# Down products one expert behind the gate and up products, loads in that order, and the last h2 rows written ahead of the last output store

## The chip, the cores and the metric

The kernel runs on one core of a Trainium2 chip. Its engines are PE (matmul), DVE (VectorE), ACT (ScalarE), POOL (GpSimd) and SP (SyncE, which here only issues transfers); each works through its own list of instructions in order and waits on semaphores for the others. Sixteen DMA engines move the data. The metric is the time of one execution on the device in microseconds, the median of the runs shown.

## The reference, cut to what matters

One layer of a streaming encoder for 512 prompt rows and 64 sample rows (576 in all, model width 1024): attention of two kinds, an output projection with its residual, and then a hierarchical mixture of experts, in which the whole change lies:

```python
h2 = RMSNorm(x) * (1 + scale2) + shift2
x  = x + gate2 * HierMoE(h2)

g_sel = argmax(n @ w_rg + b_rg)                    # one of 4 groups
e_logits = (n @ w_re + b_re).reshape(-1, 4, 8)     # 8 experts in each
top_val, top_i = top_k(e_in_group, 2)
w_top = softmax(top_val) * p_group
for e in range(32):
    act = silu(n @ w_e_gate[e]) * (n @ w_e_up[e])  # 1024 -> 256
    out = out + combine[:, e:e + 1] * (act @ w_e_down[e])   # 256 -> 1024
```

## The kernel before, in words

The rows stand in tiles of 128 (four of prompt rows, t = 0 to 3, and one of 64 sample rows). After the output projection each tile gets its residual `y[t]`, which `store_rows(t)` writes to the output `y`, and its normed rows h2, which `keep_h2(t)` writes to a scratch array `h_d` in DRAM. Both writes are issued by ACT. The router then makes, for each of 32 experts, a table of at most 64 rows: `gidx` (rows of `h_d` to gather, a column for each pair of experts), `sidx` (half rows of the output, a column for each expert) and the weights `wslot`. `weight_table` and `overflow_blocks` go on to make the table of what lies beyond 64 rows; this one goes through DVE, an IOTA on POOL and two small writes by ACT, `ov_d` and `ovf_d`.

For a pair of experts `clear_rows` (a copy on ACT) zeroes a tile `xg`, `gather_rows` (an indirect DMA that POOL issues) fetches 128 rows of `h_d`, and `turned_rows` transposes them: eight PE transposes into `pxg`, copied to `xT` in two halves, by ACT (line 90) and by DVE (line 92). For one expert there follow

- the gate and up products, tile `gu`: eight steps of four matmuls with `weg` and `weu` (line 1602);
- silu on ACT and a product on DVE, tile `sl` (lines 1606 and 1607);
- two transposes `ta` on PE and their copy `aT` on ACT (lines 1612 and 1614);
- the down products, tile `dn`, with `wed` (line 1619), times the gains `gw` (`row_gains`, lines 1593 and 1594) and added on DVE to the 128 half rows `yr`;
- `take_rows`, issued before that, gathers those half rows from the output, and `put_rows` scatters them back, both indirect DMAs of POOL (lines 1637 and 1643). A take follows in the program the writes that it may depend on, the stores of `y` among them.

Each expert has three weight tiles of 1 MB, `weg`, `weu` and `wed`. They go through a ring of 20 tiles, which is filled before the expert loop begins; `next_tile` hands out the next tile of the ring in the order expert 0's three, expert 1's three and so on, SP issues its load (line 1488), and it waits both for a free slot and for the landing of an earlier load.

The order on every engine is written by hand: the functions are called in program order, and inside the expert loop `expert_parts` is a generator that `begin` runs a few steps at a time. Of expert e+1 three steps of products run, then ta of expert e, two more steps, then dn of expert e, and then the three left of e+1. The last two tiles of `wed` are loaded together (`held`). Ahead of the loop come the gather of pair 0, `weight_table`, `overflow_blocks`, `turned_rows` of pair 0, the gather of pair 1, the takes of experts 0 and 1, and the products of expert 0.

Of the kernel before, what the change touches and what calls it, by code (L numbers as in the profile page):

```python
# [26 lines left out]
KD = 8  # L27
# [5 lines left out]
NE = 32  # L33
# [14 lines left out]
def body(ctx, tc, I, O):  # L48
# [1418 lines left out]

    shapes = (("weg", wg_, KD, FE), ("weu", wu_, KD, FE), ("wed", wd_, 2, D))
# [11 lines left out]
    def next_tile():  # L1480
        e, i = divmod(turnstile[0], 3)
        w = ring_tile(shapes[i][2], shapes[i][3], shapes[i][0])
        ahead.setdefault(e, []).append(in_halves(w, shapes[i][2]))
        return pieces_of(w, e % 4 * 8 + e // 4, i)
# [112 lines left out]
    def expert_parts(xT, w, wp, ws, yr):  # L1597
        gu = s_ps("gu")
        gw = row_gains(wp, ws)
        for k in range(KD):  # L1600
            for j in range(2):
                pe.matmul(gu[64 * j:64 * j + 64, 0:FE], xT[:, k], w[j][k // 4][:, k % 4, :],  # L1602
                          start=(k == 0), stop=(k == KD - 1))
            yield
        sl = work.tile([128, FE], F32, name="sl", tag="yh", bufs=3)
        act.activation(sl[64:128], gu[0:64, 0:FE], AF.Silu)  # L1606
        dve.tensor_mul(sl[64:128], sl[64:128], gu[64:128, 0:FE])
        yield
# [6 lines left out]
        yield  # L1615
# [33 lines left out]
    with tc.manual_schedule(engines=ENG):  # L1649
# [104 lines left out]
        store_rows(3)  # L1754
# [15 lines left out]
        keep_h2(3)  # L1770
        for _ in range(9):
            steps(chain, 1)
            steps(chain4, 1)
# [12 lines left out]
        steps(slot)  # L1786
        steps(weights)
        Z_cm.__exit__(None, None, None)
        Ep = ctx.enter_context(tc.tile_pool(name="Ep", bufs=2))
        ovrow = Ep.tile([1, 24, 4], I32, name="ovrow", bufs=1)  # L1790
        weight_table()
        overflow_blocks()
        xT = turned_rows(xg, 128)
        xg = clear_rows()
        gather_rows(xg, gidx[:, 1:2], 128)
        yrs = {e: take_rows(sidx[:, e:e + 1], e) for e in range(2)}

        def parts_of(e):
            j = 64 * (e % 2)
            return expert_parts(xT[:, :, j:j + 64], ahead[e], wslot[:, 0, e:e + 1], wslot[:, 1, e:e + 1], yrs[e])  # L1800

        e0 = parts_of(0)
        steps(e0, KD + 2)
    held = []

    def load_next(e):
        for i in range(3 * e + 20, 3 * e + 23):
            if i == 3 * (NE - 2) + 2:
                held.extend(next_tile())
            elif i == 3 * NE - 1:  # L1810
                load(held)
                load_tiles(1)
            elif i < 3 * NE:
                load_tiles(1)

    with tc.manual_schedule(engines=ENG):
        steps(e0)
        put_rows(yrs[0], sidx[:, 0:1], 0)
        load_next(0)
        begun = {0: iter(())}  # L1820
        nxt = [turned_rows(xg, 128)]

        def begin(e, n):
            nonlocal xT
            if e < NE and e not in begun:
                if e % 2 == 0:
                    xT = nxt.pop()
                begun[e] = parts_of(e)
            if e < NE:
                steps(begun[e], n)  # L1830

        def rows_ahead(e):
            if e < NE:
                yrs[e] = take_rows(sidx[:, e:e + 1], e)

        xg = clear_rows()
        gather_rows(xg, gidx[:, 2:3], 128)
        rows_ahead(2)
        begin(1, 3 + 2)
        for e in range(1, NE):  # L1840
            begin(e, KD + 1 - 3 - 2)
            begin(e + 1, 3)
            begin(e, 1)
            begin(e + 1, 2 if e < NE - 2 else KD + 1 - 3)
            begin(e, 9)
            put_rows(yrs[e], sidx[:, e:e + 1], e)
            load_next(e)
            if e == NE - 2:
                begin(e + 1, 9)
                put_rows(yrs[e + 1], sidx[:, e + 1:e + 2], e + 1)  # L1850
                break
            if e % 2 == 0:
                nxt.append(turned_rows(xg, 128))
                m = e // 2 + 2
                if m < NE // 2:
                    xg = clear_rows()
                    gather_rows(xg, gidx[:, m:m + 1], 128)
            rows_ahead(e + 2)
            if e == 8:
                act.dma_start(ovrow, ov_d[0:24].rearrange("(o a) b -> o a b", o=1))  # L1860

    nov = nc.values_load(ovrow[0:1, 0, 2:3], min_val=0, max_val=MAXOV,
                         skip_runtime_bounds_check_because="at most 1152 routed rows in blocks of 64")
    with tc.For_i(0, nov, 1) as it:
# [27 lines left out]
        steps(expert_parts(xT[:, :, 0:64], load_expert(bass.ds(ent, 1)), wsl[:, 0], wsl[:, 1], yr))  # L1892
# [49 lines left out]
```

## Time and profile before

| | us |
|---|---|
| median of 3 runs | 894.48 |
| lowest, highest | 893.54, 895.44 |
| the profiled execution | 895.09 |
| its span | 893.1 |
| PE busy in the span | 796.2 (89%) |
| DVE busy | 534.2 (60%) |
| ACT busy | 310.8 (35%) |
| POOL busy | 289.1 (32%) |

The span is what the profiler sees of the program, from its first to its last instruction; the profiled execution lasts 2.0 us longer. Its own time is 0.6 us above the median. The kernel moves 195 MB in the span, and half of that is the 96 tiles of 1024 KB of the experts' weights. The busy times are shares of the whole span, over stages of different kinds, so they don't tell what limits the experts.

### The profile page before, as it was taken

The numbers are of one execution on the slowest core, as the hardware profiler recorded it, in microseconds if no ns is written. First come the engines' busy times: TensorE is split into PE (matmuls) and PEld (weight loads), VectorE is DVE, ScalarE is ACT, GpSimd is POOL, SyncE is SP. The second block draws the span as 40 slices with busy tenths as digits, with TensorE's granted clock in tenths as the row PEclk, the third lists the DMA queues.
The fourth block names the chain that finished last, engine by engine and source line by source line (L and its number), as shares of the span: only waits on it lengthen the run. The fifth ranks groups of instructions, "written<-read, shape, count | busy, mean of one in ns | idle before, by whom it ended". The sixth has DMA issues, their size and how long they took to land.

```text
span 893.1 us, 16227 instructions
## 1 busy us (share of the span) xinstructions
PE 796.2 (89%) x6108; PEld 627.2 (70%) x6108; DVE 534.2 (60%) x1285; ACT 310.8 (35%) x754; POOL 289.1 (32%) x380
## 2 busy tenths in 40 slices
PE   6799999999899978999999999985799998878883
PEld 3567897877689967869999999984455554444441
DVE  3458999878956988647052445498355444342441
ACT  4363322475533546557232323432212212111210
POOL 1551432254447740412010103441233343332321
PEclk9899999999999989999999999996799999999997
DMA  9956778321012300126233129989699999999980
GB/s 307 344 168 217 263 242 297 104 62 61 17 61 88 108 4 2 49 97 172 71 95 95 49 97 345 350 301 405 186 415 414 413 412 407 415 413 401 416 333 36
DMA packets 78530, 194.95 MB, mean 218 GB/s; under 512 B 13587, under 2 KB 48387, under 8 KB 66419
## 3 DMA queue, kind: packets, MB, share of 16 engines
q1 hardware_dynamic: 68768, 174.85, 53.6%
q0 software_dynamic: 7424, 14.18, 4.7%
q10 hardware_dynamic: 2258, 4.87, 1.4%
q8 instruction: 49, 0.80, 0.4%
q14 instruction: 31, 0.25, 0.1%
HBM read 186.86 MB, written 18.01 MB: 229 GB/s over the span
## 4 chain that ended last, share of the span: by engine, by line
PE 46%; DMA 24%; DVE 18%; issue 5%; ACT 3%; POOL 2%; SPq 1%; POOLq 0%; DVEq 0%; ACTq 0%
DMA weu<-in_w_e_up 11%; DMA yr<-out_y,sidx 4%; PE pg L410 4%; PE pg L412 4%; PE pg L411 4%; PE gu L1602 3%; PE pj L215 3%; PE pj L217 3%; PE pj L216 3%; DVE K L904 2%; DVE acc L683 2%; DVE m L682 2%; DMA xg<-h_d,gidx 2%; DMA weg<-in_w_e_gate 2%; PE o L799 2%
## 5 line engine op out<-in xcount | busy, mean ns | idle before, releaser
L1602 PE MATMUL gu<-weu,xT 128*64 128x256 f32 x512 | 133.4, 402 | 21.7 <-DMA weu<-in_w_e_up 21.7
L1602 PE MATMUL gu<-weg,xT 128*64 128x256 f32 x512 | 132.2, 398 | 0.5 <-ACT sl L1606 0.5
L215 PE MATMUL pj<-whi,hT 128*128 128x256 f32 (+1 forms) x352 | 107.3, 305 | 0.9 <-DVE yn L472 0.6
L217 PE MATMUL pj<-whi,hT 128*128 128x256 f32 (+1 forms) x352 | 100.7, 286 | 1.3 <-DVE hT L234 1.3
L216 PE MATMUL pj<-wlo,hT 128*128 128x256 f32 (+1 forms) x352 | 100.5, 286 | 0.0
L1602 PEld LDWEIGHTS gu<-weg,xT 128*64 128x64 f32 x512 | 66.6, 141 | 40.8 <-issue 13.3
L203 DVE TENSOR_TENSOR wlo<-raw,whi 128x512 fp32r<-128x512 f32 (+1 forms) x72 | 53.5, 764 | 68.4 <-ACT whi L202 67.8
L1602 PEld LDWEIGHTS gu<-weu,xT 128*64 128x64 f32 x512 | 67.8, 142 | 33.7 <-DMA weu<-in_w_e_up 27.6
L1621 DVE TENSOR_TENSOR gw<-gw,dn 128x512 f32<-128x512 f32 x32 | 22.0, 688 | 105.6 <-PE dn L1619 105.6
L1643 POOL DMA_INDIRECT out_y<-yr,sidx x32 | 33.7, 1053 | 148.2 <-DVE yr L1622 139.2
L410 PE MATMUL pg<-hT,whi 128*128 128x256 f32 (+1 forms) x256 | 78.3, 306 | 0.0
L412 PE MATMUL pg<-hT,whi 128*128 128x256 f32 (+1 forms) x256 | 75.7, 296 | 0.0
L411 PE MATMUL pg<-hT,wlo 128*128 128x256 f32 (+1 forms) x256 | 75.7, 296 | 0.0
L215 PEld LDWEIGHTS pj<-whi,hT 128*128 128x128 f32 x352 | 67.1, 190 | 8.1 <-issue 4.9
L217 PEld LDWEIGHTS pj<-whi,hT 128*128 128x128 f32 x352 | 66.6, 189 | 1.6 <-DVE hT L234 1.5
L216 PEld LDWEIGHTS pj<-wlo,hT 128*128 128x128 f32 x352 | 66.9, 190 | 0.1
L203 POOL TENSOR_TENSOR wlo<-raw,whi 128x512 fp32r<-128x512 f32 (+1 forms) x32 | 41.9, 1332 | 74.2 <-ACT whi L202 54.4
L202 ACT CAST whi<-raw 128x512 fp32r<-128x512 f32 (+1 forms) x104 | 60.3, 624 | 14.8 <-PE pu L1134 14.8
L1619 PE MATMUL dn<-wed,aT 128*64 128x512 f32 x256 | 60.5, 594 | 0.8 <-ACT aT L1614 0.8
L410 PEld LDWEIGHTS pg<-hT,whi 128*128 128x128 f32 x256 | 48.5, 189 | 4.6 <-issue 4.3
L906 POOL TENSOR_TENSOR B<-B,K 128x512 f32<-128x512 f32 (+4 forms) x36 | 35.5, 985 | 41.5 <-DVE K L904 29.2
L411 PEld LDWEIGHTS pg<-hT,wlo 128*128 128x128 f32 x256 | 48.5, 190 | 0.2
(392 smaller groups left out, 2026.4 us busy)
## 6 DMA issues: line engine op xcount, KB each, us to landing
weg<-in_w_e_gate SPq DMA_DIRECT2D x26, 1024.0 KB, 16.5
weu<-in_w_e_up SPq DMA_DIRECT2D x26, 1024.0 KB, 21.6
wed<-in_w_e_down SPq DMA_DIRECT2D x26, 1024.0 KB, 18.5
raw<-in_w_in SPq DMA_DIRECT2D x20, 1024.0 KB, 5.6
wa<-in_w_ada SPq DMA_DIRECT2D x16, 512.0 KB, 10.6
va<-in_w_ada SPq DMA_DIRECT2D x8, 1024.0 KB, 5.3
obT<-in_w_ada SPq DMA_DIRECT2D x8, 1024.0 KB, 6.7
weg<-in_w_e_gate SPq DMA_DIRECT2D x12, 512.0 KB, 11.1
```

The source lines that it names most:

```text
L202: act.copy(hi[:, a:a + 2], raw[:, a:a + 2])
L203: eng.tensor_tensor(lo[:, a:a + 2], raw[:, a:a + 2], hi[:, a:a + 2].bitcast(F32), op=ALU.subtract)
L215: pe.matmul(p[:, :n], a, hi[:, k, :], start=(k == 0), stop=False)
L216: pe.matmul(p[:, :n], a, lo[:, k, :], start=False, stop=False)
L217: pe.matmul(p[:, :n], b, hi[:, k, :], start=False, stop=(k == KD - 1))
L410: pe.matmul(p[:, :b - a], hi[:, k, cs], hT[:, k, a:b], start=(k == 0), stop=False)
L411: pe.matmul(p[:, :b - a], lo[:, k, cs], hT[:, k, a:b], start=False, stop=False)
L412: pe.matmul(p[:, :b - a], hi[:, k, cs], hT[:, k, LP + a:LP + b], start=False, stop=(k == KD - 1))
L906: pool.tensor_tensor(B[:, :nk], B[:, :nk], K[:, 1:nk + 1], op=ALU.mult)
L1602: pe.matmul(gu[64 * j:64 * j + 64, 0:FE], xT[:, k], w[j][k // 4][:, k % 4, :], start=(k == 0), stop=(k == KD - 1))
L1619: pe.matmul(dn[64 * j:64 * j + 64, :], aT[:, k, :], w[2][k][:, 0, j * 512:(j + 1) * 512], start=(k == 0), stop=(k == 1))
L1643: ordered(pool.indirect_dma_start(out=y_rows, out_offset=bass.IndirectOffsetOnAxis(ap=idx_ap, axis=0), in_=yr, in_offset=None, bounds_chec ...
```

## The change

A list `sequence` sets the order of the ring: gate and up tiles of expert e, then the down tile of expert e-1. The generator is cut into `expert_up`, `expert_turn` and `expert_down`. The loop now runs for expert e: all products of `gu`; after an odd expert the transposes of the next pair's rows; dn and the put of expert e-1; the gains of e+1; ta of expert e; two or three loads; after an odd expert the next gather; the take of expert e+2. `held` is gone, and the loads end in the same order as before. Ahead of the loop the takes of experts 0 and 1 and the gather of pair 1 stand before `weight_table` and `overflow_blocks`, and in the program before them. `store_rows(3)` stands behind `keep_h2(3)`. Line numbers below 1468 stay, those of the helpers grow by about five.

```diff
+    sequence = [(0, 0), (0, 1)]
+    for e in range(1, NE):
+        sequence += [(e, 0), (e, 1), (e - 1, 2)]
+    sequence.append((NE - 1, 2))
...
     def next_tile():
-        e, i = divmod(turnstile[0], 3)
+        e, i = sequence[turnstile[0]]
...
-        store_rows(3)
         steps(chain, 6)
...
         xg = clear_rows()
         keep_h2(3)
+        store_rows(3)
...
         gather_rows(xg, gidx[:, 0:1], 128)
         row_indices(rowc, NE, sidx)
-        steps(slot)
-        steps(weights)
         Z_cm.__exit__(None, None, None)
...
+        yrs = {e: take_rows(sidx[:, e:e + 1], e) for e in range(2)}
+        steps(slot)
+        steps(weights)
+        xg1 = clear_rows()
+        gather_rows(xg1, gidx[:, 1:2], 128)
         weight_table()
         overflow_blocks()
         xT = turned_rows(xg, 128)
-        xg = clear_rows()
-        gather_rows(xg, gidx[:, 1:2], 128)
-        yrs = {e: take_rows(sidx[:, e:e + 1], e) for e in range(2)}
...
+        def down(e):
+            expert_down(aTs.pop(e), ahead.pop(e), gws.pop(e), yrs[e])
+            put_rows(yrs.pop(e), sidx[:, e:e + 1], e)
+
+        gain_rows(0)
+        for e in range(NE):
             j = 64 * (e % 2)
...
-        for e in range(1, NE):
-            begin(e, KD + 1 - 3 - 2)
-            begin(e + 1, 3)
-            begin(e, 1)
-            begin(e + 1, 2 if e < NE - 2 else KD + 1 - 3)
-            begin(e, 9)
-            put_rows(yrs[e], sidx[:, e:e + 1], e)
-            load_next(e)
...
+            sl = expert_up(xT[:, :, j:j + 64], ahead[e])
+            if e % 2 and e < NE - 1:
+                xT = turned_rows(xg, 128)
                 m = e // 2 + 2
                 if m < NE // 2:
                     xg = clear_rows()
-                    gather_rows(xg, gidx[:, m:m + 1], 128)
-            rows_ahead(e + 2)
+            if e:
+                down(e - 1)
+            gain_rows(e + 1)
+            aTs[e] = expert_turn(sl)
+            for _ in range(2 if e == 0 else 3):
+                if turnstile[0] < len(sequence):
+                    load_tiles(1)
+            if e % 2 and e < NE - 1 and m < NE // 2:
+                gather_rows(xg, gidx[:, m:m + 1], 128)
+            if e + 2 < NE:
+                yrs[e + 2] = take_rows(sidx[:, e + 2:e + 3], e + 2)
...
+        down(NE - 1)
```

POOL, at the entry to the expert stage. Its list before (`xg<-h_d` is a gather, `yr<-out_y` a take, `out_y<-yr` a put, `IOTA rq` the step of `overflow_blocks`):

```order
L1573 DMA xg<-h_d,gidx 128x1024
L1555 IOTA rq 128x32
L1573 DMA xg<-h_d,gidx 128x1024
L1637 DMA yr<-out_y,sidx 128x512 x2
L1643 DMA out_y<-yr,sidx 1152x512
```

And after, at the same place:

```order
L1578 DMA xg<-h_d,gidx 128x1024
L1644 DMA yr<-out_y,sidx 128x512 x3
L1578 DMA xg<-h_d,gidx 128x1024
L1560 IOTA rq 128x32
L1650 DMA out_y<-yr,sidx 1152x512
```

Three takes and the gather of pair 1 have moved ahead of the IOTA, on which the issues of `ov_d` and `ovf_d` depend.

ACT, in the same stretch, before (`R` is a step of the router's softmax, `xg<-zero` is `clear_rows`):

```order
L1411 ACTIVATE R<-R 128x5
L1564 DMA ov_d<-ovi 128x4
L1565 DMA ovf_d<-ovf 128x1
L90 COPY xT<-pxg 128x512
L1569 COPY xg<-zero_82 128x1024
L1606 ACT_TABLE_LOAD
```

And after:

```order
L1411 ACTIVATE R<-R 128x5
L1574 COPY xg<-zero_82 128x1024
L1569 DMA ov_d<-ovi 128x4
L1570 DMA ovf_d<-ovf 128x1
L90 COPY xT<-pxg 128x512
L1609 ACT_TABLE_LOAD
```

The zeroing of pair 1's tile has moved ahead; the copy of `xT` for expert 0 still stands behind the two small writes.

PE, near the end, before, with buffer numbers: the last row of the products of expert 30 (`gu_9364`), the first six of expert 31 (`gu_9405`), and ta of expert 30:

```order
L1602 MATMUL gu_9364<-weu_9086,xT_9338 64x256
L1602 MATMUL gu_9405<-weg_9131,xT_9338 64x256
L1602 MATMUL gu_9405<-weu_9133,xT_9338 64x256
L1602 MATMUL gu_9405<-weg_9131,xT_9338 64x256
L1602 MATMUL gu_9405<-weu_9133,xT_9338 64x256
L1602 MATMUL gu_9405<-weg_9131,xT_9338 64x256
L1602 MATMUL gu_9405<-weu_9133,xT_9338 64x256
L1612 MATMUL ta_9414<-ident_72,sl_9402 128x64 x2
```

And after: the last row of the products of expert 30 (`gu_9375`), dn of expert 29, ta of expert 30, and the first two rows of the products of expert 31 (`gu_9412`):

```order
L1606 MATMUL gu_9375<-weu_9059,xT_9341 64x256
L1626 MATMUL dn_9395<-wed_9105,aT_9369 64x512 x2
L1626 MATMUL dn_9395<-wed_9106,aT_9369 64x512 x2
L1617 MATMUL ta_9407<-ident_72,sl_9392 128x64 x2
L1606 MATMUL gu_9412<-weg_9109,xT_9341 64x256
L1606 MATMUL gu_9412<-weu_9111,xT_9341 64x256
```

So ta of expert 30 no longer stands among the products of expert 31, whose sixteen rows now stand in one piece. In both kernels dn of expert 30, ta and dn of expert 31 follow them and end the list.

## Rows read from the trace of the kernel before

**Rows 1.** Windows: length; PE, PEld, DVE, ACT, POOL busy (x); clock; DMA share; GB/s.
```profile
600.00:625.00 25.00, 13.89 (x133) 12.64 (x133) 21.70 (x108) 6.58 (x14) 6.28 (x8) 0.68 1.00 404
...
650.00:850.00 200.00, 177.45 (x1198) 94.16 (x1196) 86.92 (x143) 36.55 (x78) 71.48 (x65) 0.97 1.02 412
```

**Rows 2.** Waits from 600 us: us in total, times, longest us.
```profile
PE gu L1602 <- DMA weu<-in_w_e_up: 21.7, 11, 3.1
```

**Rows 3.** Timeline of SP's issues: start, us, line, transfer.
```profile
638.10 0.33 SPq L1488 DMA_DIRECT2D wed<-in_w_e_down  x1
...
856.06 0.33 SPq L1488 DMA_DIRECT2D wed<-in_w_e_down  x1
```

**Rows 4.** Timeline of PE, products of expert 0, first and last two pairs.
```profile
632.54 0.69 PE L1602 MATMUL gu<-weg,xT 128*64 128x256 f32 x1
...
637.48 0.38 PE L1602 MATMUL gu<-weg,xT 128*64 128x256 f32 x1
...
637.69 0.38 PE L1602 MATMUL gu<-weg,xT 128*64 128x256 f32 x1
```

**Rows 5.** Timeline of PE, the tail: end of the last weu wait, ta, dn.
```profile
870.89 0.43 PE L1602 MATMUL gu<-weu,xT 128*64 128x256 f32 x1 [1.02 <-DMA weu<-in_w_e_up]
...
872.34 0.45 PE L1612 MATMUL ta<-ident,sl 64*128 64x64 f32 x2
872.72 0.43 PE L1602 MATMUL gu<-weg,xT 128*64 128x256 f32 x1
...
874.93 1.89 PE L1619 MATMUL dn<-wed,aT 128*64 128x512 f32 x8
```

**Rows 6.** Timeline of ACT, with its DMA issues (ACTq).
```profile
605.03 0.33 ACTq L1331 DMA_DIRECT2D h_d<-h2k  x1
...
611.03 0.34 ACTq L1647 DMA_DIRECT2D out_y<-y  x1
...
613.94 1.04 ACT L1569 COPY xg<-zero 128x1024 f32<-128x1024 f32 x1 [1.99 <-DMA h_d<-h2k]
614.72 0.33 ACTq L1331 DMA_DIRECT2D h_d<-h2k  x1
...
630.83 0.33 ACTq L1564 DMA_DIRECT2D ov_d<-ovi  x1
...
631.87 0.59 ACT L90 COPY xT<-pxg 128x512 f32<-128x512 f32 x1 [8.44 <-PE pxg L1582]
```

**Rows 7.** Timeline of POOL: gather, IOTA, takes, and expert 30's put.
```profile
624.61 1.28 POOL L1573 DMA_INDIRECT xg<-h_d,gidx  x1 [11.99 <-DVE rhs L1442]
629.84 0.20 POOL L1555 IOTA rq<- 128x32 f32 x1 [3.96 <-DVE rq L1550]
...
635.02 1.01 POOL L1637 DMA_INDIRECT yr<-out_y,sidx  x1 [0.30 <-issue]
636.33 1.00 POOL L1637 DMA_INDIRECT yr<-out_y,sidx  x1 [0.30 <-issue]
...
878.55 1.02 POOL L1643 DMA_INDIRECT out_y<-yr,sidx  x1 [6.02 <-DVE yr L1622]
```

**Rows 8.** Timeline of DVE, second step of the gains of expert 0.
```profile
633.77 0.75 DVE L1594 SCALAR_TENSOR_TENSOR gw<-gate,wslot,gw 128x512 f32<-128x512 f32 x1
```

**Rows 9.** Windows of 3 us around the first loads, columns as in rows 1.
```profile
631.00:634.00 3.00, 3.00 (x16) 2.11 (x16) 1.32 (x3) 2.11 (x3) 0.32 (x1) 0.50 0.05 1
...
637.00:640.00 3.00, 1.68 (x14) 0.90 (x12) 0.42 (x1) 0.64 (x2) 0.33 (x1) 1.00 0.42 49
640.00:643.00 3.00, 2.35 (x13) 0.93 (x12) 0.69 (x1) 0.00 (x0) 0.00 (x0) 1.00 0.72 215
643.00:646.00 3.00, 3.00 (x29) 2.04 (x29) 2.44 (x4) 1.53 (x2) 1.29 (x2) 1.00 1.02 429
```

**Rows 10.** The page: queue of POOL's transfers, and the gathers' us to landing.
```profile
q0 software_dynamic: 7424, 14.18, 4.7%
...
xg<-h_d,gidx POOLq DMA_INDIRECT x16, 9.0
```

More of the change, by code (lines that the diff above doesn't have):

```diff
@@ L1480, in next_tile @@
     def next_tile():
-        e, i = divmod(turnstile[0], 3)
+        e, i = sequence[turnstile[0]]
         w = ring_tile(shapes[i][2], shapes[i][3], shapes[i][0])
-        ahead.setdefault(e, []).append(in_halves(w, shapes[i][2]))
+        ahead.setdefault(e, [None] * 3)[i] = in_halves(w, shapes[i][2])
         return pieces_of(w, e % 4 * 8 + e // 4, i)
@@ L1595, in row_gains, with expert_up @@
         return gw
-    def expert_parts(xT, w, wp, ws, yr):
+    def expert_up(xT, w):
         gu = s_ps("gu")
-        gw = row_gains(wp, ws)
         for k in range(KD):
@@ L1603, in expert_parts @@
                           start=(k == 0), stop=(k == KD - 1))
-            yield
         sl = work.tile([128, FE], F32, name="sl", tag="yh", bufs=3)
@@ L1607, in expert_parts, with expert_turn @@
         dve.tensor_mul(sl[64:128], sl[64:128], gu[64:128, 0:FE])
-        yield
+        return sl
+    def expert_turn(sl):
         av = sl.rearrange("s (p k) -> s k p", k=2)
@@ L1614, in expert_parts, with expert_down @@
         act.copy(aT, ta[:, 0:128].rearrange("p (k c) -> p k c", k=2))
-        yield
+        return aT
+    def expert_down(aT, w, gw, yr):
         dn = s_ps("dn")
@@ L1793, in body @@
         xT = turned_rows(xg, 128)
-        xg = clear_rows()
-        gather_rows(xg, gidx[:, 1:2], 128)
-        yrs = {e: take_rows(sidx[:, e:e + 1], e) for e in range(2)}
-        def parts_of(e):
-            j = 64 * (e % 2)
[L1800 to L1839, printed above, removed]
-        for e in range(1, NE):
-            begin(e, KD + 1 - 3 - 2)
-            begin(e + 1, 3)
-            begin(e, 1)
-            begin(e + 1, 2 if e < NE - 2 else KD + 1 - 3)
-            begin(e, 9)
-            put_rows(yrs[e], sidx[:, e:e + 1], e)
-            load_next(e)
[L1848 to L1853, printed above, removed]
@@ new lines, in body, with gain_rows @@
+        xg = xg1
+    with tc.manual_schedule(engines=ENG):
+        gws, aTs = {}, {}
+        def gain_rows(e):
+            if e < NE:
+                gws[e] = row_gains(wslot[:, 0, e:e + 1], wslot[:, 1, e:e + 1])
+        def down(e):
[3 more added lines that the diff above has]
+        for e in range(NE):
+            j = 64 * (e % 2)
+            sl = expert_up(xT[:, :, j:j + 64], ahead[e])
+            if e % 2 and e < NE - 1:
+                xT = turned_rows(xg, 128)
@@ L1891, in body @@
         yr = take_rows(idi[:, 0:1])
-        steps(expert_parts(xT[:, :, 0:64], load_expert(bass.ds(ent, 1)), wsl[:, 0], wsl[:, 1], yr))
+        w = load_expert(bass.ds(ent, 1))
+        gw = row_gains(wsl[:, 0], wsl[:, 1])
+        expert_down(expert_turn(expert_up(xT[:, :, 0:64], w)), w, gw, yr)
         put_rows(yr, idi[:, 0:1])
```

## Prediction

> **What bounds the kernel now.** I read the windows of the last third first. From 650 to 850 us the DMA engines are full (share 1.02, 412 GB/s), while PE, at a granted clock of 0.97, is busy 177 of 200 us [rows 1]. The waits say what it stands for: loads of weu, 21.7 us [rows 2]. So the expert stage runs at the pace of its loads. SP's own list shows where that pace begins: the ring is full, and nothing is issued until the first slots come free at 638.10, when PE is through with the gate and up products of expert 0; the last load leaves at 856.06 [rows 3]. Of 96 loads 20 are ahead, so 76 go out in 218 us, 2.87 us each: two experts, six loads, take 17.2 us. PE's work for two experts is 12.7 us: 2 x 16 pairs of products at 0.21, two dn of 1.89, two ta of 0.45 and a pxg that I take at 1.1, since it holds eight matmuls as dn does, of a quarter of the columns [rows 4, 5]. What is done on PE in the steady part is hidden under the loads. Only three things can move the time: the moment at which loading resumes, what slows the first loads, and the tail behind the last load.
>
> **Part 1, the order inside the loop.** The down products move one expert back. Matmuls and loads are the same in number, and the two slots that the first two loads need, those of weg0 and weu0, come free when the products of expert 0 end, as before. In the steady part I cost the new order at nothing: the loads cover it, by 17.2 less 12.7, 4.5 us per pair, and if that cover were gone each us more would cost 14 us, one per pair. In the tail it shortens the path. Before, the transposes ta of expert 30 stand among the gate and up products of expert 31, behind their wait for the last weu (870.89): ta at 872.34, the next product at 872.72, then dn30 at 874.93 [rows 5]. After, ta(30) stands ahead of those products and their wait, so dn30, ta31, dn31 and the last put come 0.38 us earlier. **Term: -0.4** (0 if the landing of wed30 or wed31 is late next; -0.8 if ACT's copy behind ta, now long done, had held dn30 by as much again).
>
> **Part 2, h_d(3) ahead of the y(3) store.** Both stand on ACT's queue and hold 0.52 MB. h_d(2) went out at 605.03, with no store shortly ahead, and its landing released ACT at 613.94: 8.9 us. h_d(3) went out at 614.72, the y(3) store 3.69 us ahead of it, and the gather that needs it issued at 624.61: at most 9.9 us [rows 6, 7]. So gather(0) comes up to 1.0 us earlier, which alone is worth nothing, as part 3 shows what is late next. The store now goes out at some 615.1 instead of 611.03.
>
> **Part 3, the early takes and what they push.** Before, POOL issues gather(0) at 624.61, makes the IOTA for the overflow table at 629.84, and only then gather(1) and the first takes [rows 7]. After, it issues gather(0), three takes and gather(1), and then makes the IOTA. Two things follow. Four DMA issues stand ahead of the IOTA, at a pitch of 1.31 (635.02 to 636.33). And the first take reads out_y, so it waits for the landing of the y(3) store, and everything on POOL is queued behind it. That landing has no row. Early end: h_d's flight of 8.9 from 615.1 is 624.0. Late end: served wholly behind h_d(3), its 0.52 MB at a third of the 404 GB/s that the stretch moves [rows 1] need 3.9 us from 624.6: 628.5. I take 627.2, nearer the late end, because the DMA engines are full there and the store is the last in its queue. So: takes at 627.2, 628.5 and 629.8, gather(1) at 631.1, IOTA at 632.4, +2.6 against before.
> Behind the IOTA stands a DVE step, behind that ACT's issues of ov_d and ovf_d, and behind these on ACT's queue its copy of xT for expert 0. Before: IOTA 629.84, ov_d 630.83, xT copy 631.87, first product 632.54 [rows 4, 6, 7]. The copy then waited for pxg; after, pxg has long ended and the copy follows ovf_d, for which I take off 0.2: first product at 634.9, **+2.4**. Low end +1.1: the store lands before the first take's turn, so that the takes start at 625.9 and the IOTA at 631.1. That also covers the DVE side, where gain_rows(0), steps of at most 0.75 [rows 8], now stands in the same chain. High end +3.7, with a landing at 628.5.
> **The granted clock.** It is 0.50, the lower of the two levels, when the products of expert 0 begin, and 1.00 when they end; the 16 pairs take 5.5 us (632.54 to 638.1), where 16 at the upper pitch of 0.21 would take 3.4 and 16 at twice that 6.8 [rows 4, 9]. PE now pauses for over two us between pxg and the first product. I take two more pairs at the lower level: **+0.4** (-0.4 for two fewer, +1.3 for all 16). Loading then resumes at 638.10 + 2.8 = 640.9 (638.8 to 643.1).
> **What comes back.** Before, gather(1) and two takes, issued until 636.33, still run when the first loads go out. The windows from 637 show 49, 215 and 429 GB/s [rows 9]. Against 412 the one from 640 to 643 loses 3 x (1 - 215/412) = 1.4 us, and the stretch from 638.1 to 640 at most 1.9 x (1 - 49/412) = 1.7, of which an unknown part is the loads' own start. After, those transfers are issued by 631.1 and over before 640.9. I take 1.4 and somewhat under half of the rest: **-2.1** (-1.4 to -3.1). The totals give the same size: queue q0 fills 4.7% of 893.1 us, 42 us, 2.6 us for each of 16 pairs of experts [rows 10], of which a gather and two of its four 128x512 takes and puts are about two thirds, 1.75, and the third take, moved too, another 0.4: 2.2.
> The Trainium skill ("DMA: Bandwidth & Descriptors", section Issuing engines are not separate DMA queues) says that DMAs started by SP, ACT and GpSimd run on the same 16 engines and interleave. The windows agree: weights come at half rate beside a gather. By the rule the whole time of the moved transfers, 2.2, comes back, and the sum would be 0.1 less; if POOL's transfers had engines of their own it would be 2.1 more.
>
> **Sum.** -0.4 + 2.4 + 0.4 - 2.1 = +0.3 on the profiled execution of 895.09, which is 895.4. The median of the three runs, 894.48, is 0.6 below that execution, so I predict **894.8**. What a measurement of this kernel can tell from no change is about 0.2%, 1.8 us: 892.7 to 896.3 counts as the same.
>
> **Rivals.**
> A, slower: nothing is given back, because the slow start at 638 is the loads' own, and the chain POOL, IOTA, ov_d, xT delays the resumption by its full length. It decides from a landing of the y(3) store after 626.5. Price +2.4 to +3.7, clock +0.4, tail -0.4: +2.4 to +3.7, 896.9 to 898.2, about 897.4. For it: four issues stand ahead of the IOTA in any case. Against it: 215 GB/s just where the gather still runs [rows 9].
> B, faster: h_d(3), freed of the store, lands a us earlier or more, and the store right behind it; POOL's chain starts at 623.6, the IOTA comes at 630.2, the first product is late by 0.2 to 1.1, the clock costs nothing, the whole 3.1 comes back, and the tail gives 0.4 to 0.8: -2.4 to -3.7, about 891.6. Against it: h_d(2) took 8.9 with nothing ahead, and the DMA engines are full there.
> The Trainium skill (the same page, section Queues, rings and completion order) says that on each DMA engine the descriptors of one queue are consumed in ring order: the write put first is served first, as B needs, and the store is served last, as A needs. The 8.9 against 9.9 us show at most 1.0 of it.
> C, slower: gather(m) is now issued behind put(e-1) and its rows are needed two experts on. From one pxg to the next stand pxg 1.1, dn to the put's issue 3.6 (874.93 to 878.55 [rows 5, 7]), the gather 1.3 later, and its flight of 9.0 [rows 10]: 15.0 us, under the 17.2 of the loads. With a flight of 12 it binds, and each half us over costs 14 x 0.5 = 7 us: some 900. Only a flight a third longer speaks for it.
>
> **How the numbers follow.** The forecast, terms within their bounds, 892.7 to 896.3: 0.55. A 0.22 and C 0.03: slower by over 0.2%, 0.25. B 0.20: faster by over 0.2%. The range runs from B's 891.6 to A's upper half, 897.8; C and the last of A lie outside.
>
> **What would show it.** In the profile after: the IOTA at 632.4 and ov_d near 633.4; the first product at 634.9, its pairs at the lower level until about 638.8; SP's first load at 640.9, and 400 GB/s within two us of it, with no gather beside it; the last load's issue at 856 to 857; PE still waiting for weu, and a share of 1.02, in the steady part; dn30 some 3.7 us behind the last wait for weu, 4.0 before. The prediction fails if loading resumes outside 638.8 to 643.1, if the steady windows move clearly other than 412 GB/s, or if PE waits for xg there.

## The result: slower, 907.6 us

| | before | after |
|---|---|---|
| median, us | 894.96 (893.54 to 896.62, 4 runs) | 907.62 (906.55 to 908.12, 4 runs) |
| the profiled execution | 895.09 | 907.3 |
| its span | 893.1 | 905.4 |
| first load of the expert stage | 638.10 | 640.65 |
| last put | 881.28 | 893.63 |

The ratio is 1.0131 (95% interval 1.0112 to 1.015): 12 us slower, outside the range of 891.6 to 897.8. Two more measurements of the changed kernel gave 906.12 and 906.62.

The entry to the stage came out much as forecast. POOL, ACT, PE and SP of the kernel after, in the timelines (start, us, engine, line, operation, what it waited for), which answer to [rows 3, 4, 6, 7]:

```profile
625.35 1.28 POOL L1578 DMA_INDIRECT xg<-h_d,gidx  x1 [11.39 <-DVE val L1413]
627.71 1.01 POOL L1644 DMA_INDIRECT yr<-out_y,sidx  x1 [1.08 <-DMA out_y<-y]
...
632.73 0.23 POOL L1560 IOTA rq<- 128x32 f32 x1
```

```profile
633.76 0.33 ACTq L1569 DMA_DIRECT2D ov_d<-ovi  x1
...
634.69 0.58 ACT L90 COPY xT<-pxg 128x512 f32<-128x512 f32 x1 [8.96 <-DVE xT L92]
```

```profile
635.32 0.69 PE L1606 MATMUL gu<-weg,xT 128*64 128x256 f32 x1 [3.22 <-ACT xT L90]
```

```profile
640.65 0.33 SPq L1493 DMA_DIRECT2D weg<-in_w_e_gate  x1
```

The first take waits for the y(3) store until 627.71, the IOTA comes at 632.73, the first product at 635.32, the first load at 640.65, 2.55 us later than before. In the traces of the two later measurements of the changed kernel it leaves at 640.03 and 639.22, so a trace by itself fixes such a moment to a microsecond or so. The other ten microseconds are lost after that. The waits of the kernel after, from 600 us on (us in total, times, longest), which answer to [rows 2]:

```profile
PE pxg L1587 <- DMA xg<-h_d,gidx: 36.4, 15, 3.5
```

There is no row of PE waiting for weu any more; before it had 21.7 us of them. PE now waits for the gathered rows, at all 15 gathers that the loop uses. Four windows of the kernel after (columns as in [rows 1]):

```profile
650.00:700.00 50.00, 41.38 (x268) 20.76 (x264) 19.24 (x32) 8.17 (x17) 16.00 (x15) 0.90 1.02 415
700.00:750.00 50.00, 43.90 (x315) 23.74 (x316) 22.92 (x38) 9.08 (x20) 18.35 (x18) 0.96 0.95 379
750.00:800.00 50.00, 41.25 (x269) 22.54 (x267) 20.08 (x33) 8.06 (x17) 14.75 (x14) 0.90 1.02 414
800.00:850.00 50.00, 43.08 (x283) 22.24 (x280) 20.32 (x33) 8.43 (x18) 16.59 (x16) 0.90 1.02 413
```

In three of the four the DMA engines are as full as before, at the same rate (the four of before have 413, 414, 411 and 409 GB/s), and the granted clock is 0.90, where before it was 1.00, 0.99, 0.94 and 0.93. The stretch with 379 GB/s is taken up below. Full DMA engines and a PE that never waits for a weight go together here: the loads run ahead of their use, out of the stock in the ring. The last one is issued by 854.1, the last dn starts at 889.95, 36 us later; before it was 21.5 us.

How the rounds run is read from POOL's gathers. The kernel before, gathers of pairs 2, 9 and 15:

```profile
645.73 1.08 POOL L1573 DMA_INDIRECT xg<-h_d,gidx  x1 [0.31 <-issue]
...
741.26 1.02 POOL L1573 DMA_INDIRECT xg<-h_d,gidx  x1 [0.31 <-issue]
...
847.27 1.02 POOL L1573 DMA_INDIRECT xg<-h_d,gidx  x1 [0.31 <-ACT sl L1606]
```

The kernel after, pairs 2 and 15:

```profile
651.72 1.03 POOL L1578 DMA_INDIRECT xg<-h_d,gidx  x1 [0.31 <-issue]
...
864.61 1.03 POOL L1578 DMA_INDIRECT xg<-h_d,gidx  x1 [0.31 <-issue]
```

Call the time from one of these gathers to the next a round; it holds the work for one pair of experts. Before, there are seven rounds of 13.6 us on the average (645.73 to 741.26), while the stock of 20 tiles in the ring is used up, and then six of 17.7, at the pace of the loads: 15.5 on the average of 13. After, there are 13 rounds of 16.4 on the average (212.9 us against 201.5). So the gather of pair 2 comes 6.0 us later, the 13 rounds take 11.4 longer, and from the last gather to the last put it takes 5.0 less (29.0 against 34.0), since the weights are there long before: 12.4 us, the whole difference of the last puts.

One round of the kernel after, the gather at 816.64, shows what it is made of. POOL:

```profile
816.64 1.02 POOL L1578 DMA_INDIRECT xg<-h_d,gidx  x1 [0.31 <-issue]
...
831.48 1.14 POOL L1650 DMA_INDIRECT out_y<-yr,sidx  x1 [7.71 <-DVE yr L1629]
832.92 1.02 POOL L1578 DMA_INDIRECT xg<-h_d,gidx  x1 [0.31 <-issue]
```

PE in the same round, and the dn of the other expert of the pair for comparison:

```profile
817.27 1.89 PE L1626 MATMUL dn<-wed,aT 128*64 128x512 f32 x8
...
825.17 1.09 PE L1587 MATMUL pxg<-ident,xg 128*128 128x128 f32 x8 [2.03 <-DMA xg<-h_d,gidx]
826.20 3.54 PE L1626 MATMUL dn<-wed,aT 128*64 128x512 f32 x8
```

And the windows around PE's wait, the last of them over that second dn alone:

```profile
822.00:825.00 3.00, 1.14 (x12) 0.47 (x8) 0.42 (x1) 0.38 (x1) 1.06 (x2) 1.00 1.04 408
825.00:828.00 3.00, 2.83 (x14) 1.49 (x16) 0.69 (x1) 1.53 (x2) 0.00 (x0) 0.73 1.03 421
828.00:831.00 3.00, 3.00 (x18) 1.04 (x16) 1.19 (x2) 0.27 (x1) 0.00 (x0) 0.70 1.02 418
...
826.20:829.70 3.50, 3.50 (x10) 0.71 (x9) 0.69 (x1) 1.20 (x2) 0.00 (x0) 0.53 1.02 414
```

Gather to pxg 8.53 us, pxg to dn 1.03, dn to put 5.28 (dn itself 3.54, then two steps on DVE), put to the next gather 1.44: 16.28, and then it begins again. Every part waits for the one before, so this is a closed loop. It closes because PE now transposes the next rows ahead of dn of expert e-1, and POOL issues the next gather behind that expert's put: the put waits for dn, dn stands behind pxg, pxg waits for the gather in flight. Before, dn and its put stood ahead of pxg, and the put that the next gather follows owed nothing to the gather in flight. In its wait for the rows PE is idle, the granted clock of the windows falls from 1.00 to about 0.7, and the dn that follows takes 3.54 instead of 1.89 us. Over this dn the clock is 0.53, so nearly all of it runs at the lower of the two levels. The wait so lengthens the loop that makes it wait. The 13 rounds of this trace say the same: in the three shortest (14.63, 14.82 and 15.19) the dn behind the wait took 1.94 us, in the ten others (16.18 to 17.79) between 2.66 and 3.54.

### The profile page after: what moved, and what is told of

Same layout as the page of the kernel before. It is cut to its first block, busy times and chain, and to the rows that moved or that the text cites. A ratio compares the mean times of both kernels' runs of the same rounds, so it can differ in the third digit from the quotient of the medians.

```text
span 905.4 us, 16239 instructions
## 1 busy us (share of the span) xinstructions
PE 800.8 (88%) x6108; PEld 628.9 (69%) x6108; DVE 535.8 (59%) x1285; ACT 310.8 (34%) x754; POOL 286.2 (32%) x380
## 4 chain that ended last, share of the span: by engine, by line
PE 37%; issue 23%; DVE 17%; POOL 9%; DMA 8%; ACT 3%; SPq 1%; POOLq 0%; DVEq 0%; ACTq 0%
PE pg L410 4%; PE pg L411 4%; PE pg L412 4%; POOL yr L1644 3%; PE pj L215 2%; DMA out_y<-yr,sidx 2%; DVE K L904 2%; POOL out_y L1650 2%; DVE acc L683 2%; DMA out_y<-y 2%; DVE m L682 2%; PE pj L216 2%; PE pj L217 2%; PE o L799 2%; DVE wlo L203 2%
## 5 line engine op out<-in xcount | busy, mean ns | idle before, releaser
L1606 PE MATMUL gu<-weg,xT 128*64 128x256 f32 x512 | 119.1, 386 | 3.2 <-ACT xT L90 3.2
L1606 PE MATMUL gu<-weu,xT 128*64 128x256 f32 x512 | 119.1, 387 | 0.0
L1650 POOL DMA_INDIRECT out_y<-yr,sidx x32 | 36.1, 1129 | 163.4 <-DVE yr L1629 163.4
L1626 PE MATMUL dn<-wed,aT 128*64 128x512 f32 x256 | 75.5, 721 | 0.4 <-ACT aT L1619 0.4
L1587 PE MATMUL pxg<-ident,xg 128*128 128x128 f32 x128 | 21.2, 318 | 36.4 <-DMA xg<-h_d,gidx 36.4
L1610 DVE TENSOR_TENSOR sl<-sl,gu 64x256 f32<-64x256 f32 x32 | 13.6, 424 | 60.9 <-ACT sl L1609 60.9
```

The source lines that it names most:

```text
L1650: ordered(pool.indirect_dma_start(out=y_rows, out_offset=bass.IndirectOffsetOnAxis(ap=idx_ap, axis=0), in_=yr, in_offset=None, bounds_chec ...
```

## Experiments: is it the loop?

Two theories: the closed loop; or a stop of SP. SP's waits after show one that is new (640 to 905 us):

```profile
SPq L1493 <- DMA ovrow<-ov_d: 12.9, 1, 12.9
```

It stood from 697 to 710 us behind ACT's small read of the overflow table, and the windows from 705 to 714 show 265, 151 and 268 GB/s, 4 us of loads lost. That is the stretch with 379 GB/s above.

**The loop cut at the gather.** Behind `xg = clear_rows()`, and no longer behind the put:

```diff
                 if m < NE // 2:
                     xg = clear_rows()
+                    gather_rows(xg, gidx[:, m:m + 1], 128)
             if e:
                 down(e - 1)
...
-            if e % 2 and e < NE - 1 and m < NE // 2:
-                gather_rows(xg, gidx[:, m:m + 1], 128)
```

> The changed kernel, with the gather of pair m issued right behind the zeroing of its tile, so ahead of the put of expert e-1. Theory 1 (a closed loop: gather, its flight, pxg, dn, two DVE steps, put, next gather, 16.4 us per pair in the trace after): the loop opens, since the gather no longer waits for the put of the expert whose dn stands behind pxg; PE waits for weu again, no longer for xg, and the time is 893 to 898, ten or more less than the changed kernel's 907.6. Theory 2 (the 13 us for which SP stood behind the read of the overflow table): nothing is done to it, 905 to 909.

Measured: 894.98, ratio to before 0.9997 (0.9982 to 1.0012). All of the loss is gone with one line moved. PE's waits in it, from 640 us:

```profile
PE gu L1606 <- DMA weu<-in_w_e_up: 19.5, 12, 2.8
...
PE pxg L1587 <- DMA xg<-h_d,gidx: 0.2, 1, 0.2
```

**The loop cut at the transposes.**

```diff
             sl = expert_up(xT[:, :, j:j + 64], ahead[e])
+            if e:
+                down(e - 1)
             if e % 2 and e < NE - 1:
                 xT = turned_rows(xg, 128)
...
-            if e:
-                down(e - 1)
```

> The changed kernel, with the transposes of the next pair's rows behind dn and put of expert e-1 instead of ahead of them; the gather stays behind the put. Theory 1: the other side of the same loop is cut, since dn and put no longer wait for the gather that is in flight; 893 to 899. Theory 2: 905 to 909. If the put ahead of the gather costs by itself on POOL, and not through the loop, this stays slow and e1 is fast.

Measured: 895.44, ratio 1.0 (0.9985 to 1.0014). The put ahead of the gather costs nothing where dn does not stand behind pxg: it is the loop, and not an issue too many on POOL.

**The other theory: the table read late.**

```diff
-            if e == 8:
+            if e == 26:
                 act.dma_start(ovrow, ov_d[0:24].rearrange("(o a) b -> o a b", o=1))
```

> The changed kernel, with ACT's read of the overflow table issued at expert 26, behind the last of SP's loads, instead of at expert 8. Theory 1: SP's stop of 13 us goes and the DMA engines lose no 4 us at 705 to 714, but PE had weights ahead all the time, so 906 to 908. Theory 2: the stop is the cause, and the time falls by 4 (what the DMA engines lost) to 13 (the length of the stop): 895 to 904.

Measured: 902.71 (901.07 to 905.01), ratio 1.0081 (1.0053 to 1.0108). That is under the 906 to 908 of the loop alone and inside the 895 to 904 forecast for the other theory, though far from the whole loss. It was repeated, with the changed kernel beside it, measured twice in all:

> The changed kernel itself, beside the other runs of this call, for the read of the overflow table at expert 26 (902.7 in the earlier call). If that gain of some five us is real, this comes out at 906 to 909; if it was the chip of that call, at 902 to 904.

> The changed kernel with the overflow table read at expert 26, beside the changed kernel itself in the same call. If SP's stop of 13 us behind that read costs time in the closed loop, this is 3 to 5 us under it; theory 1 alone says the same within 1.5 us.

> The changed kernel itself, for the comparison with the run before it in this call: 905 to 908.

Measured: 906.12 for the changed kernel in one comparison; 904.64 (901.7 to 906.2) with the late read and 906.62 (904.17 to 908.89) without in the other. The ratios there are 1.0103 (1.0085 to 1.012) and 1.0134 (1.0117 to 1.0151): two microseconds, with intervals that just overlap.

But reading the table late did not take the stop away, it moved it and made it longer. SP in the first run with the late read, its waits and the issues on both sides of the stop:

```profile
SPq L1493 <- DMA ovrow<-ov_d: 25.6, 1, 25.6
...
825.44 3.48 SPq L1493 DMA_DIRECT2D weg<-in_w_e_gate  x2
854.55 0.33 SPq L1493 DMA_DIRECT2D weu<-in_w_e_up  x1
```

SP stands from 829 to 854.55, twice as long as in the changed kernel, and the run is no slower for it: PE never waits for a weight there either. So these runs are no test of a kernel without the stop, but they show that the stop does not make the ten microseconds. What they gain lies in the loop. The gather of pair 14 goes out in the stop, while few loads are on their way:

```profile
849.64 1.03 POOL L1578 DMA_INDIRECT xg<-h_d,gidx  x1 [0.31 <-issue]
...
856.19 1.09 PE L1587 MATMUL pxg<-ident,xg 128*128 128x128 f32 x8
...
857.21 1.94 PE L1626 MATMUL dn<-wed,aT 128*64 128x512 f32 x8
```

From its issue to pxg it takes at most 6.55 us, where the 14 gathers from pair 2 on take 8.5 to 10.0 in the trace of the changed kernel. PE does not wait, dn takes 1.94 us, and this round 12.7 us (12.6 in the repetition, with at most 6.43 for the gather), where the same round takes 15.19 in the trace of the changed kernel. That would account for what these runs gain. A loop with no such stop at all is in the run with the loop alone in the kernel before, further down: there SP never waits for this read, and it is as slow, 904.49.

**The loop made longer.** The gather behind the take, too:

```diff
-            if e % 2 and e < NE - 1 and m < NE // 2:
-                gather_rows(xg, gidx[:, m:m + 1], 128)
             if e + 2 < NE:
                 yrs[e + 2] = take_rows(sidx[:, e + 2:e + 3], e + 2)
+            if e % 2 and e < NE - 1 and m < NE // 2:
+                gather_rows(xg, gidx[:, m:m + 1], 128)
```

> The changed kernel, with the gather of pair m behind the take of expert e+2 instead of ahead of it: one more issue of 1.3 us in the loop of theory 1, in each of 13 rounds. Theory 1: slower by 17 (13 x 1.3) to 30 (where the take also waits): 924 to 938. Theory 2, or a stage bound by its loads: no change, 905 to 910.

Measured: 921.26, ratio 1.0294 (1.0258 to 1.033). The round grew from 16.4 to 17.7 us, by the 1.3 of one issue, and 13 x 1.3 = 17 was expected; 14 came. It fell just under the stated 924, because from the last gather to the last put it took 23.9 us instead of 29.0: the loads were over by then (83 GB/s from 883 to 889), and the last gather needed 5.09 us to pxg.

**The loop alone, in the kernel before.**

```diff
+            if e % 2 == 0 and e < NE - 2:
+                nxt.append(turned_rows(xg, 128))
+                m = e // 2 + 2
+                if m < NE // 2:
+                    xg = clear_rows()
             begin(e, 9)
             put_rows(yrs[e], sidx[:, e:e + 1], e)
             load_next(e)
...
-            if e % 2 == 0:
-                nxt.append(turned_rows(xg, 128))
-                m = e // 2 + 2
-                if m < NE // 2:
-                    xg = clear_rows()
-                    gather_rows(xg, gidx[:, m:m + 1], 128)
+            if e % 2 == 0 and m < NE // 2:
+                gather_rows(xg, gidx[:, m:m + 1], 128)
```

> The kernel before, with one move in its expert loop: at even experts the transposes of the next rows, and the zeroing behind them, stand ahead of dn and put of expert e, and the gather stays behind the put. The order of loads, the entry and the rest are those of before. Theory 1 (the closed loop of gather, flight, pxg, dn, put, gather): 16 to 16.5 us per pair, gathers at that pitch from the first pairs on, and 903 to 910. Theory 2 (the slowness comes from the new order of loads or from the entry): 894 to 897.

Measured: 904.49, ratio 1.0098 (1.0061 to 1.0135), rounds of 16.4 us. With the old order of loads and the old entry, the loop alone makes the kernel slow; neither the new order of loads nor the new entry is needed for it.

**The entry alone, in the kernel before.** The diff is the one shown with the change, from `store_rows(3)` to `xg = xg1`.

> The kernel before with the two parts of the change ahead of the loop: the y(3) store behind h_d(3), takes of experts 0 and 1 and gather of pair 1 ahead of the weight table and the overflow table. The loop and the order of loads are those of before. By the prediction's terms (+2.4, +0.4, -2.1) it comes out within 2 us of before; first product 2 to 3 us later, first load by as much. If the first loads' slow start is their own and not the gather's, +2 to +4.

Measured: 894.54, ratio 0.9985 (0.9971 to 0.9998). The first load leaves at 640.59. The entry is worth a microsecond gained, if anything, although loading resumes later.

**The wait filled with work.**

```diff
             if e % 2 and e < NE - 1:
+                fill = s_ps("gu")
+                for k in range(6):
+                    for h in range(2):
+                        pe.matmul(fill[64 * h:64 * h + 64, 0:FE], xT[:, k, j:j + 64],
+                                  ahead[e][h][k // 4][:, k % 4, :], start=(k == 0), stop=(k == 5))
                 xT = turned_rows(xg, 128)
```

> The changed kernel, with 24 more products (six steps of expert e's own, into a tile that nobody reads, 2.6 us by its trace) ahead of the transposes of the next rows, so that PE works while it would wait for the gather. Nothing is left out. In the trace after, the granted clock falls to 0.61 behind that wait and dn takes 3.4 instead of 1.9 us, in the loop. Theory 1 with the clock as part of the loop: dn back at 1.9, loop 16.4 - 1.5 = 14.9 us, time 893 to 899 in spite of the added work. Theory 1 with a loop that is only as long as the flight: 905 to 909, or more by what the products stick out.

Measured: 896.12, ratio 1.0004 (0.9993 to 1.0015): ten microseconds faster than the changed kernel (906.12 in the same comparison), with more work on PE. Windows and dn of this run at the same place of a round:

```profile
816.00:819.00 3.00, 3.00 (x30) 1.83 (x25) 0.42 (x1) 0.38 (x1) 0.93 (x1) 1.00 1.02 405
819.00:822.00 3.00, 3.00 (x18) 1.41 (x16) 0.93 (x2) 1.53 (x2) 0.00 (x0) 1.00 1.05 406
```

```profile
819.77 1.94 PE L1626 MATMUL dn<-wed,aT 128*64 128x512 f32 x8
```

PE is busy all the time, the clock stays at 1.00, dn is back at 1.9 and the round takes 15.4. PE's own work now fills nearly the whole round: 2.6 us for the 24 products, and 12.5 for the rest (the prediction's list of it adds up to 12.5, not to its 12.7). So the lower clock behind the wait was what made the loop longer than the loads allow: with a dn of 1.9 the 16.28 above would be 14.6. The Trainium skill ("TensorE: Matmul & The Clock Gate", section Loop structure matters more than you think) says that the loop nest decides whether matmuls stay at the upper level, and that a long wait for a DMA inside it loses it; these two traces agree, 0.70 behind the wait and 1.00 without it.

The round, first gather of the loop to the last over 13, against the time:

| kernel | round, us | median, us |
|---|---|---|
| gather ahead of the put | 14.9 | 894.98 |
| transposes behind dn | 15.1 | 895.44 |
| filled wait | 15.4 | 896.12 |
| before | 15.5 | 894.96 to 895.65 |
| after, table read late | 16.1 to 16.2 | 902.71 to 904.64 |
| before, transposes ahead | 16.4 | 904.49 |
| after | 16.4 to 16.5 | 906.12 to 907.62 |
| gather behind the take | 17.7 | 921.26 |

Up to 15.5 a round costs nothing: it is the average that the loads themselves give. Beyond that a microsecond in the round costs some ten to fifteen, about one for each of the 13 rounds.

## Experiments: what slows the first loads?

The prediction had given the slow start of the first loads to the gather beside them. The next two runs begin loading earlier.

**The transposes for expert 0 ahead of the overflow table**, on the run with the gather ahead of the put:

```diff
         weight_table()
-        overflow_blocks()
         xT = turned_rows(xg, 128)
+        overflow_blocks()
```

> The changed kernel with the gather ahead of the put (as in the first run), and with the transposes for expert 0 ahead of the overflow table, so that ACT's copy of xT no longer stands behind ov_d and ovf_d. The prediction's chain (IOTA, ov_d, xT, first product: +2.4) says that the first product comes 2 to 3 us earlier than in that run, the first load too, and the time is 891 to 894; if other parts bind the entry, 894 to 896.

Measured: 897.07, ratio 1.002 (1.0006 to 1.0033), above both forecasts. The step came off, first product at 629.91 and first load at 635.07, 4.5 us earlier than in the run with the gather ahead of the put alone (639.58), and no time was gained. Windows of this run:

```profile
637.00:640.00 3.00, 3.00 (x31) 1.75 (x27) 0.25 (x1) 0.00 (x0) 0.00 (x0) 1.00 0.96 394
640.00:643.00 3.00, 3.00 (x19) 1.45 (x18) 1.12 (x3) 1.91 (x3) 0.51 (x1) 1.00 2.11 292
643.00:646.00 3.00, 3.00 (x28) 2.07 (x30) 2.61 (x4) 0.27 (x1) 1.66 (x2) 1.00 0.80 35
646.00:649.00 3.00, 3.00 (x22) 1.26 (x18) 0.73 (x2) 0.38 (x1) 1.04 (x1) 1.00 0.48 22
```

The loads reach nearly the full rate within two microseconds and then all but stop; with the window behind these, 300 GB/s, seven microseconds of loads are lost. It is not for want of loads: SP issues them in the same steps as in the run with the gather ahead of the put, only earlier (635.07, 635.49, 640.08, 640.53, 642.99 against 639.58, 640.00, 644.59, 645.04, 647.50), and that run shows 421 and 369 GB/s from 643 to 649. In the stop the DMA engines have a share of 0.80 and 0.48 while they move 35 and 22 GB/s. Ahead of it, at 635.18 and 635.61, ACT issued the two writes of the overflow table, 128 pieces of 16 bytes and 128 of 4.

**PE kept at work ahead of the first transposes**, besides:

```diff
+        fill = s_ps("gu")
+        for k in range(5):
+            for h in range(2):
+                w0 = ahead[0][0][h]
+                pe.matmul(fill[64 * h:64 * h + 64, 0:FE], w0[:, k % 4, 0:64], w0[:, k % 4, :],
+                          start=(k == 0), stop=(k == 4))
         xT = turned_rows(xg, 128)
         overflow_blocks()
```

> The run before, with ten products more on PE (five steps with weights of expert 0, into a tile that nobody reads) ahead of the transposes of the first rows, so that PE works while it waits for the first gather. Nothing is left out. If the lower clock of expert 0's products is due to PE standing before them, they take 3.5 to 4.5 instead of 5.5 us, loading resumes 1 to 2 us earlier and the time falls by as much: 889 to 893. If not, the time of the run before, or 1 more.

Measured: 896.68, ratio 1.002 (1.0007 to 1.0033). The products of expert 0 took 3.7 us (631.35 to the first load at 635.05) instead of 5.2, as forecast; the time forecast for it, 889 to 893, did not come. ACT stood at the same two writes until 636.6, and its silu came only at 637.91. Nothing came of it.

**The small writes cut**, from 128 rows to the 24 that are read, in the run with the early transposes:

```diff
-        act.dma_start(ov_d, ovi)
-        act.dma_start(ovf_d, ovf[:, 1:2])
+        act.dma_start(ov_d[0:24], ovi[0:24])
+        act.dma_start(ovf_d[0:24], ovf[0:24, 1:2])
```

> The run with the transposes for expert 0 ahead of the overflow table (897.1), with the two small writes cut from 128 rows to the 24 that are read. If the small writes are what holds the DMA engines at the first loads, the stop at 642 to 650 us goes, the earlier resumption counts, and the time is 889 to 893. If gather and takes hold them, or the loads' own start, 895 to 898.

Measured: 889.84, ratio 0.994 (0.9926 to 0.9954): faster than both kernels, by 5.4 us against before in the same comparison. Its windows:

```profile
637.00:640.00 3.00, 2.30 (x20) 1.66 (x22) 1.66 (x3) 0.46 (x2) 0.00 (x0) 1.00 0.71 221
640.00:643.00 3.00, 3.00 (x28) 1.92 (x25) 0.61 (x2) 1.00 (x3) 0.00 (x0) 1.00 1.00 421
643.00:646.00 3.00, 3.00 (x20) 1.36 (x18) 1.78 (x3) 1.17 (x2) 1.02 (x1) 1.00 1.01 153
646.00:649.00 3.00, 3.00 (x30) 1.85 (x28) 1.34 (x3) 0.30 (x1) 2.18 (x2) 1.00 1.01 426
```

The stop has shrunk to some two microseconds, with the loads issued in the same steps (636.76, 637.18, 641.78, 642.22, 644.68).

**The same cut in the kernel before, and in the run with PE at work:**

> The kernel before with the two small writes cut from 128 rows to 24, and nothing else. Small writes: full rate 2 to 4 us earlier than at 643, time 892 to 894. Gather beside the first loads, as the prediction had it: no change, 894.5 to 896.

> The run with ten products more ahead of the first transposes (896.7), with the two small writes cut to 24 rows. Small writes: 889 to 893, and not above the run without the ten products. Otherwise 895 to 898.

Measured: 894.42, ratio 0.9986 (0.9975 to 0.9997), and 893.49, ratio 0.9981 (0.9972 to 0.999). In the kernel before the cut is worth a microsecond at most, between the two forecasts, and the full rate does not come 2 to 4 us earlier: the windows from 637 show 152, 292 and 367 GB/s, where before they show 49, 215 and 429. In the kernel before the writes go out at 630.83, seven microseconds ahead of the first load, so that part of their stop can fall into the time without loads; that is argued, not shown. The ten products of the other run cost more than they bring, 3.7 us against the run without them, and it missed its forecast of not coming out above that run; its silu of expert 0 again came late, behind ACT's writes (638.80).

**The small writes made twice:**

```diff
+            if e == 14:
+                act.dma_start(ov_d, ovi)
+                act.dma_start(ovf_d, ovf[:, 1:2])
```

> The first run (gather ahead of the put, 895.0), with the two small writes of 128 rows made a second time at expert 14, where the DMA engines are full. Small writes: a stop of 5 to 8 us in the loads there, and 899 to 903. Otherwise 256 short pieces beside 80,000 packets: 894 to 896.

Measured: 897.74, ratio 1.0033 (1.002 to 1.0045), 2.8 us above the run without; less than forecast. The writes go out at 730.26 and 730.70. Windows of this run:

```profile
734.00:737.00 3.00, 3.00 (x18) 1.31 (x18) 1.66 (x3) 1.76 (x3) 1.03 (x1) 1.00 1.01 391
737.00:740.00 3.00, 3.00 (x32) 1.97 (x30) 1.98 (x4) 0.04 (x1) 2.03 (x2) 1.00 1.34 272
740.00:743.00 3.00, 2.38 (x14) 0.83 (x10) 1.34 (x3) 0.64 (x2) 1.03 (x1) 1.00 0.74 67
743.00:746.00 3.00, 0.65 (x2) 0.19 (x2) 1.70 (x3) 0.00 (x0) 1.14 (x1) 1.00 0.84 294
```

The run without the second writes shows 407, 408, 408 and 427 GB/s there. The stop comes seven to ten microseconds behind the issue, as in the run above, and takes 4.6 us of loads (3 x (16/407 + 136/408 + 341/408 + 133/427)). A part of it is SP's: in this run it stands 5.3 us, until 743.65, behind the landing of the second write, with fewer loads on their way meanwhile. So the small writes hold up the loads. Where loading begins early they are most of what held it; in the kernel before they are at most a microsecond of its slow start, and how the rest is shared between the gather and a start of the loads' own was not told apart.

## Why the prediction was wrong, step by step

- **What bounds the kernel.** "The expert stage runs at the pace of its loads", 17.2 us per pair, was read from a window of 200 us and from a total of waits. It holds for the second half only. The 20 tiles ahead let PE run at 13.6 for seven pairs, so that over 13 rounds the loads allow one of 15.5. POOL's timeline of the kernel before shows it; I had read it only at its entry. PE's sum was off too, without consequence: 2 x 16 x 0.21 + 2 x 1.89 + 2 x 0.45 + 1.1 is 12.5.
- **Part 1, the step that failed.** "In the steady part I cost the new order at nothing: the loads cover it, by 17.2 less 12.7, 4.5 us per pair." The cover was 15.5 less the length of whatever chain is longest, and the new order made a chain of 16.3. PE's sum of work, 12.7, was not the thing to compare. The prediction's own last sign of failing, "if PE waits for xg there", is what came: 15 waits, 36.4 us.
- **Rival C named the mechanism and its sum was mis-sized twice.** It had pxg 1.1, dn to put 3.6, gather 1.3, flight 9.0: 15.0. Measured in the round shown: 1.03, 5.28, 1.44, 8.53: 16.28. The error is in dn to put, 1.7 us too short, taken from a dn at the upper clock; behind a wait it runs nearly all at the lower one. The gather, 0.5 shorter than assumed, makes up for a part of it. And the bound was put at 17.2 instead of 15.5. With both right the rival says 13 x (16.3 - 15.5) = 10 us, most of the 12 measured. It had a chance of 0.03 because "Only a flight a third longer speaks for it". (By its own rule a flight of 12 would make the round 0.8 too long, which is 11 us and some 906, not 900.)
- **Part 2, the order of the two writes: no gain seen.** gather(0) was to come up to 1.0 us earlier and came 0.74 later, at 625.35, with h_d(3) issued 1.35 later (616.07) and the store at 616.45 instead of 615.1. In both traces the gather waits last for a step of DVE, so nothing shows that it stood behind h_d(3) at all. The sum is not touched, since this term stood at nothing.
- **Part 3, the entry: right, with some luck in the decimals.** First take behind the store at 627.71 (taken 627.2), IOTA 632.73 (632.4), first product 635.32 (634.9), first load 640.65 (640.9). In the two later traces of the changed kernel the first product comes at 634.32 and 632.80, and the products of expert 0 take 5.7 and 6.4 us, in this one 5.3, against 5.6 before: the clock term of +0.4 lies within that scatter. The entry alone gave 894.54, within the 2 us stated.
- **What comes back, right in size, its cause only in part.** From the first load to the full rate, in windows of 1 us, it took 4.9 us before (638.10 to 643) and about 3.4 after (640.65 to 644; 3.0 and 2.8 in the two later traces), so 1.5 to 2.1 came back, where 2.1 was taken. But the gather was not the only cause: with the gather where it was, cutting the small writes gained up to a microsecond in the kernel before, and the run with the early start gained 7 by the same cut.
- **The Trainium skill's two rules** ("DMA: Bandwidth & Descriptors"). That transfers of all engines share the 16 DMA engines agrees: ACT's writes hold up SP's loads, 35 and 22 GB/s in two windows. That a queue is consumed in ring order fits the y(3) store landing by 627.71, behind h_d(3), which the gather could read at 625.35, but since the store was also issued later, no run tests the rule. The landing is past the 626.5 at which rival A was to decide, and yet A's price of 2.4 to 3.7 was not paid: the entry alone gave 894.54.
- **The tail of -0.4: right where it can be seen.** In the changed kernel the end no longer stood at the last load; from dn30 to dn31 it took 2.67 us in both kernels. In the run with the gather ahead of the put it stands there again. Its last wait for weu and its last put:

```profile
868.97 0.43 PE L1606 MATMUL gu<-weu,xT 128*64 128x256 f32 x1 [1.28 <-DMA weu<-in_w_e_up]
...
878.82 0.98 POOL L1650 DMA_INDIRECT out_y<-yr,sidx  x1 [1.72 <-DVE yr L1629]
```

  That is 9.85 us, where before it was 10.39 (870.89 to 881.28): 0.5 less.

## What to carry to other kernels

When a step is moved, look for chains that return to themselves (a transfer, its use, what that releases, the next transfer), add up one round at the clock that PE will have behind its wait, and compare it with the pace of the other resource averaged from the point at which its buffers are full, not with its pace when they are empty. To open such a loop it was enough here to issue the next transfer before the work that its predecessor's landing holds up.

## What the hardware showed that was not expected

- A wait of 2 to 3.5 us per pair on PE cost twice, once as a wait and once as clock: 24 products that nobody reads, put into the wait, made the kernel ten microseconds faster.
- Two writes of 128 pieces of 16 and 4 bytes held up the loads for several microseconds, beginning some 7 us behind their issue: 35 and 22 GB/s in two windows instead of 410. The Trainium skill ("DMA: Bandwidth & Descriptors", Specifications) gives 512 B as the least transfer for line rate, with a read-modify-write below that; no run here shows what the stop consists of, only that it shrinks when 24 rows are written instead of 128.
- A gather of 128 rows took 7.9 to 10.1 us from its issue to the transposes in two traces of the changed kernel, mostly beside full loads, and at most 6.55, 6.43 and 5.09 us where few loads were on their way. So the loads lengthen a loop that goes through a gather, even when PE waits for none of them.
